# A diffusion trunk on one core: the opening stage taken by quarters of the features instead of halves

## The chip, the cores and the metric

One NeuronCore of a Trainium2 chip runs the whole program. The metric is the device time of one execution in microseconds. TensorE (PE, with its weight loads as PEld), VectorE (DVE), ScalarE (ACT), GpSimd (POOL) and SyncE (SP, which issues the transfers here) each run their own list of instructions in the order in which the kernel writes them.

## The reference

Two layers run over 256 latent and 256 context tokens of 1024 features. Each sub-layer normalises its input, multiplies by a gain that depends on the condition, and adds a shift that depends on it. The first sub-layer is a gated feed-forward block. What the change touches, cut to its core:

```
lat = x + pos_embed ; cx = ctx
mod = silu(cond) @ w_ada[l] + b_ada[l]            # 9 vectors of 1024; 0 is a shift, 1 a scale
h   = rmsnorm(x, g) * (1 + mod[1]) + mod[0]        # for latents (c) and for context (c_ctx)
y   = (silu(h @ w1) * (h @ w3)) @ w2               # w1, w3: 1024 x 2816
x   = x + 0.5 * mod[2] * y
```

## The kernel before

Activations lie features by tokens: eight feature tiles of 128 partitions, 512 tokens wide (latents, then context). Products are made at nearly full float32 accuracy from three passes: `h` and each weight are split into a rounded part (`hi`, by ACT, line 210 for weights) and the rest (`lo`, by DVE, line 214), and `mm3` runs hi*hi (line 309), hi*lo (line 310) and lo*hi (line 311). One pass is one matmul of a 128x128 block on 512 tokens.

A weight item is a block of 512 rows (four feature tiles) by 256 columns. A plan lists all items in order; the function `pump` moves three counters along that list. An item is loaded when one of 3 raw buffers (`wraw`) is free, that is when the item three places before it has been split; it is split when one of 4 pairs `whi`, `wlo` is free, that is when TensorE has finished the item four places before it. Two caps, `cap_load` and `cap_split`, hold the counters back during the opening. Item 0 and item 1 are the first 512 rows of the first column blocks of w1 and w3 (the plan swaps two entries for this), items 2 and 3 the last 512 rows of the same blocks, items 4 and 5 the next column block of w1, items 6 and 7 that of w3. SP issues all transfers one after the other, and each waits for the one eight places before it on SP's list, so at most eight are under way. From a point set by `paces` on, columns of `w_ada` for later sub-layers come along with the weight items and are summed on DVE.

The first shift and scale cannot come that way, since everything waits for them. The function `start` loads their columns itself, in tiles named `a`: eight transfers of 1 MB, four for features 0 to 511 (two for the shift, `j` = 0, two for the scale, `j` = 1) and four for features 512 to 1023. `first_ada` sums one half of one vector on TensorE (line 281, into `ada_ps`), ACT copies the sum (`ada_sb`, line 284), TensorE turns it by a transpose (`ada_t`, line 290), and DVE adds the bias (line 294) and, for the scale, applies the norm's gain (line 299). The reciprocal norm of each token is spread over a diagonal (`tmp`, line 379) and broadcast to all partitions by a matmul with ones (line 386); line 985 copies it to `bcs`. `modulated(half)` then makes `h` for four feature tiles: for each tile, latents then context, DVE multiplies (line 405), ACT adds the shift and rounds (`h_hi`, line 406), DVE takes the rest (`h_lo`, line 395).

The rest of `start`, and the head of `ffn`, hold the first column block of w1 and w3: 32 groups of three passes. They come as w1 with the first half of the features (8 groups), the sums of the second half's scale, w3 with the first half (inside which the sums of the second half's shift and the making of its `h` are called as a task in the background, `second_half`), then, in `ffn`, w1 and w3 with the second half. The four PSUM buffers of the pool `mm` hold the four results (two column tiles of w1, two of w3). When a result of w1 is complete, ACT takes its silu (line 447), which frees the buffer; DVE multiplies with w3's (line 449). `turn` transposes rows of biases and gains into columns; `turn(0)` is needed for the first shift, `turn(1)` not before the second layer.

Of the kernel before, what the change touches and what calls it, by code (L numbers as in the profile page):

```python
# [74 lines left out]
class Trunk:  # L75
# [28 lines left out]
    def plan(self):  # L104
# [32 lines left out]
        paces = {(0, 1): (2, (2, 2, 2, 2, 0)), (0, 2): (4, (2, 1, 2, 1, 2, 0)), (1, 1): (4, (2, 1, 2, 1, 2, 0)),  # L137
                 (1, 2): (4, (1, 0))}
        r = []
        seen = {}  # L140
# [284 lines left out]
    def ffn(self, l, n, both):  # L425
# [6 lines left out]
        with tc.tile_pool(name=f"g{l}{n}", bufs=1) as gp:  # L432
# [31 lines left out]
            if self.begun:  # L464
                hs = self.begun
                self.begun = None
                for part, w in ((1, w1), (3, w3)):
                    it = self.take(w, l, 4, 0)
                    self.fm(it, hs[part], self.h_hi, self.h_lo, BOTH, KT)
                    self.done(it)  # L470
                    gate(hs[part], 0, whole, part)
            elif both:
                its = {0: None}
                up(0, LAT, its, keep=True)
                self.drain()
                up(0, CTXC, its)
            else:
                self.drain()
                up(0, LAT, None)
# [388 lines left out]
    def start(self):  # L868
# [23 lines left out]
        with self.tc.tile_pool(name="start", bufs=1) as st:  # L892
# [33 lines left out]
            def load_ada(half, j):  # L926
                for k in (0, 4):
                    raw = raws[half, j, k] = st.tile([P, 4, 512], F32, tag=f"a{half}{j}{k}", name="a0")
                    c0 = j * D + 512 * half
                    src = io["w_ada"][0, k * P:(k + 4) * P, c0:c0 + 512]  # L930
# [12 lines left out]
            while small:  # L943
                nc.sync.dma_start(*small.pop(0))
            self.cap_load = len(self.ws)
# [1 line left out]

            cond = st.tile([P, KT, 32], F32, tag="cond", name="cond0")
            nc.vector.memset(cond, 0.0)
            bcs = self.wp.tile([P, 2, 512], F32, tag="acc", name="bcs")  # L950
            ss = self.sp.tile([P, 16], F32, tag="ss", name="ss", bufs=3)[:, :2]

            def enter(s, k2):
                a, b = (LAT, CTXC)[s]
                w = SEQ // GRID_W
                ps = (self.aux, self.bank)[s]()
                for k in (k2, k2 + 1):
                    for t in range(2):
                        o = SEQ * (k - k2) + t * P
                        nc.tensor.transpose(ps[:, o:o + P], xs[("x", "ctx")[s]][:, t, k * P:(k + 1) * P], self.ident)  # L960
                if s == 1:
                    nc.scalar.activation(self.x[:, k2:k2 + 2, a:b], ps.rearrange("p (k t) -> p k t", k=2), AF.Copy)
# [10 lines left out]
                for k in (k2, k2 + 1):  # L973
                    self.add_square(k, (a, b))

            def first_ada(half, j):
                self.ada_rows(0, j, half, [(cond[:, k], raws[half, j, 4 * (k // 4)][:, k % 4]) for k in range(KT)])

            def finish_ada():
                later, self.later = self.later, []  # L980
                for f in later:
                    f()

            def row(s, dg):
                nc.vector.tensor_copy(bcs[:, s, :SEQ], self.broadcast(dg))

            def modulated(half):
                for _ in self.modulate(0, 0, [bcs[:, s, :SEQ] for s in range(2)],
                                       [[(s, k) for k in range(4 * half, 4 * half + 4) for s in range(2)]]):
                    pass  # L990

            for k2 in range(0, KT, 2):
                enter(0, k2)
                if k2 == 2:
                    ps = self.bank()
                    nc.tensor.transpose(ps[:, :16], cc, self.ident[:16, :16])
                    nc.scalar.activation(cond[:, :, 0:2], ps[:, :16].rearrange("p (s k) -> p k s", s=2), AF.Silu)
            for k2 in range(0, KT, 2):
                enter(1, k2)
            r = self.token_rstd(LAT)  # L1000
            for t in range(2):
                nc.scalar.activation(bcs.rearrange("p s n -> p (s n)"), xs["ctx"][:, t], AF.Square,
                                     accum_out=ss[:, t:t + 1])
            first_ada(0, 0)
            dg = [self.spread(r), self.spread(self.rstd(ss, 2, D))]
            nc.vector.tensor_copy(self.cond, cond[:, :, 0:2])

            def turn(l):
                vr, n = rows[l]
                ps = self.aux()  # L1010
                nc.tensor.transpose(ps[:, :n], vr[:n, :], self.ident[:n, :n])
                nc.vector.tensor_copy(self.vec[l][:, :n], ps[:, :n])

            turn(0)
            row(0, dg[0])
            row(1, dg[1])
            finish_ada()
            self.cap_split = 1
            self.pump()
            first_ada(0, 1)  # L1020
            finish_ada()
            modulated(0)
            self.cap_split = 2

            def second_half():
                first_ada(1, 1)
                finish_ada()
                self.cap_split = 3
                self.pump()
                modulated(1)  # L1030
                self.cap_split = len(self.ws)
                self.pump()
                yield 2
                turn(1)

            hs = {}
            for part in (1, 3):
                if part == 3:
                    first_ada(1, 0)
                    finish_ada()  # L1040
                    self.behind(second_half())
                hs[part] = [self.bank(), self.bank()]
                it = self.take(f"ffn1_w{part}", 0, 0, 0)
                self.fm(it, hs[part], self.h_hi, self.h_lo, BOTH, KT)
                self.done(it)
            self.begun = hs

    def final(self):
        nc = self.nc
# [56 lines left out]
```

## Time and profile before

| what | value |
|---|---|
| three runs | 1787.40, 1790.61, 1796.05 us, median 1790.61 |
| the profiled execution's own time | 1787.99 us |
| its span in the trace | 1786.2 us, so 1.8 us lie around it |
| TensorE busy | 1753.0 us, 98% |
| DVE, ACT busy | 63%, 38% |

Busy TensorE is close to the whole span, so what another engine saves is worth nothing unless TensorE waits for it. The three runs lie 8.7 us apart, 0.5% of the time.

### The profile page before, as it was taken

What the parts mean: (1) busy time and instruction counts of PE and PEld (TensorE: products, weight loads), DVE (VectorE), ACT (ScalarE), POOL (GpSimd) and SP (SyncE); (2) the same over time, 40 slices, a digit from 0 to 9 for tenths busy, and PEclk for the clock granted to TensorE, in tenths of its full rate; (3) what the DMA queues carried; (4) which work ended last, traced back from release to release, by engine and by line L of the source; (5) the groups of instructions that cost most, each with busy time, mean ns of one, the idle gap of its engine ahead of it and who ended that gap; (6) DMA issues with size and microseconds to landing.
All of it is one profiled execution on the core that took longest, in us unless ns stands there. A gap on an engine that the chain in (4) does not pass through costs nothing. (4 is left out here: it accounts for less than half of the span.)

```text
span 1786.2 us, 27050 instructions
## 1 busy us (share of the span) xinstructions
PE 1753.0 (98%) x10853; PEld 1534.5 (86%) x10853; DVE 1129.6 (63%) x1746; ACT 670.5 (38%) x1087; POOL 19.6 (1%) x26
## 2 busy tenths in 40 slices
PE   6999999999999999999999999999999999989998
PEld 5788888899899898888888898888888999979998
DVE  4876676775737667666666676555545668665554
ACT  3422222236545344222222252223222565545543
POOL 0000000000000000000000000000000000000000
PEclk9999999999999999999999999999999999989999
DMA  8565655664212114555555545555454532446663
GB/s 315 166 177 162 178 160 165 180 188 139 71 60 83 60 60 144 151 157 160 151 153 158 178 137 157 161 154 159 156 167 153 160 107 83 130 125 195 194 186 128
DMA packets 230646, 266.65 MB, mean 149 GB/s; under 512 B 10369, under 2 KB 192377, under 8 KB 230521
## 3 DMA queue, kind: packets, MB, share of 16 engines
q1 hardware_dynamic: 230520, 264.93, 48.8%
q8 instruction: 85, 1.39, 0.3%
q14 instruction: 41, 0.33, 0.1%
HBM read 263.84 MB, written 1.05 MB: 148 GB/s over the span
## 5 line engine op out<-in xcount | busy, mean ns | idle before, releaser
L309 PE MATMUL mm<-h_hi,whi 128*128 128x512 f32 (+1 forms) x2016 | 704.2, 349 | 4.7 <-ACT h_hi L406 3.0
L310 PE MATMUL mm<-h_lo,whi 128*128 128x512 f32 (+1 forms) x2016 | 696.8, 346 | 1.7 <-DVE h_lo L395 1.4
L311 PE MATMUL mm<-h_hi,wlo 128*128 128x512 f32 (+1 forms) x2016 | 694.1, 344 | 0.0
L214 DVE TENSOR_TENSOR wlo<-wraw,whi 128x1024 fp32r<-128x1024 f32 x362 | 430.8, 1196 | 320.0 <-ACT whi L210 318.9
L210 ACT ACTIVATE whi<-wraw 128x1024 fp32r<-128x1024 f32 x362 | 370.9, 1032 | 393.3 <-PE mm L310 271.5
L309 PEld LDWEIGHTS mm<-h_hi,whi 128*128 128x128 f32 x2016 | 380.5, 189 | 56.3 <-ACT h_hi L406 4.0
L310 PEld LDWEIGHTS mm<-h_lo,whi 128*128 128x128 f32 x2016 | 380.8, 189 | 50.7 <-DVE h_lo L395 6.0
L311 PEld LDWEIGHTS mm<-h_hi,wlo 128*128 128x128 f32 x2016 | 380.7, 189 | 47.2
L272 DVE SCALAR_TENSOR_TENSOR acc<-wada,cond,acc 128x512 f32<-128x512 f32 x392 | 275.7, 748 | 35.5 <-DMA wada<-in_w_ada_dram 33.9
L309 PE MATMUL mm<-g_hi,whi 128*128 128x256 f32 (+1 forms) x836 | 279.9, 335 | 0.0
L311 PE MATMUL mm<-g_hi,wlo 128*128 128x256 f32 (+1 forms) x836 | 276.7, 331 | 0.0
L310 PE MATMUL mm<-g_lo,whi 128*128 128x256 f32 (+1 forms) x836 | 276.7, 331 | 0.0
L309 PEld LDWEIGHTS mm<-g_hi,whi 128*128 128x128 f32 x836 | 157.3, 188 | 18.3 <-issue 2.4
L311 PEld LDWEIGHTS mm<-g_hi,wlo 128*128 128x128 f32 x836 | 157.2, 188 | 15.8
L310 PEld LDWEIGHTS mm<-g_lo,whi 128*128 128x128 f32 x836 | 157.1, 188 | 15.2
L210 ACT ACTIVATE g_hi<-silu 128x512 fp32r<-128x512 f32 (+1 forms) x92 | 51.7, 562 | 179.2 <-DVE silu L449 179.2
L447 ACT ACTIVATE silu<-mm 128x512 f32<-128x512 f32 (+1 forms) x92 | 48.2, 527 | 134.3 <-PE mm L311 134.3
L214 DVE TENSOR_TENSOR g_lo<-silu,g_hi 128x512 fp32r<-128x512 f32 (+1 forms) x92 | 55.7, 606 | 57.8 <-ACT g_hi L210 57.8
L449 DVE TENSOR_TENSOR silu<-silu,mm 128x512 f32<-128x512 f32 (+1 forms) x92 | 55.0, 598 | 28.6 <-PE mm L311 28.5
L309 PE MATMUL mm<-whi,h_hi 128*128 128x256 f32 x224 | 64.0, 286 | 0.0
L310 PE MATMUL mm<-wlo,h_hi 128*128 128x256 f32 x224 | 62.3, 278 | 0.0
L311 PE MATMUL mm<-whi,h_lo 128*128 128x256 f32 x224 | 62.2, 278 | 0.0
(128 smaller groups left out, 1055.1 us busy)
## 6 DMA issues: line engine op xcount, KB each, us to landing
wraw<-in_ffn_w_dram SPq DMA_DIRECT2D x271, 512.0 KB, 4.5
wada<-in_w_ada_dram SPq DMA_DIRECT2D x256, 256.0 KB, 3.0
wraw<-in_w_in_dram SPq DMA_DIRECT2D x56, 512.0 KB, 4.0
a<-in_w_ada_dram SPq DMA_DIRECT2D x8, 1024.0 KB, 9.8
wraw<-in_w_out_dram SPq DMA_DIRECT2D x16, 512.0 KB, 4.1
wraw<-in_ffn_w_dram SPq DMA_DIRECT2D x19, 256.0 KB, 2.7
x<-in_x_dram SPq DMA_DIRECT2D x2, 512.0 KB
ctx<-in_ctx_dram SPq DMA_DIRECT2D x2, 512.0 KB, 5.6
```

The costliest lines, as they stand in the source:

```text
L210: self.nc.scalar.activation(hi, src, AF.Copy)
L214: self.nc.vector.tensor_tensor(lo, src, hi.bitcast(F32), op=ALU.subtract)
L272: nc.vector.scalar_tensor_tensor(acc[:, s], raw, c, acc[:, s], op0=ALU.mult, op1=ALU.add)
L309: mm(ps, lhsT=l_hi, rhs=r_hi, start=start, stop=False)
L310: mm(ps, lhsT=l_hi, rhs=r_lo, start=False, stop=False)
L311: mm(ps, lhsT=l_lo, rhs=r_hi, start=False, stop=stop)
L447: nc.scalar.activation(silu[j], ps, AF.Silu)
L449: nc.vector.tensor_tensor(silu[j], silu[j], ps, op=ALU.mult)
```

## The change

The columns of the first shift and scale are loaded, summed and applied for two feature tiles at a time: sixteen transfers of 512 KB in four quarters in place of eight of 1 MB in two halves. One sum of TensorE (`quarter_sums`, line 982) now holds shift and scale of a quarter. The products of the first column block are cut along the features, so that all four results grow together: in each quarter 2 groups for the first column tile of w1, the sums of the next quarter, 2 groups for the second tile, the transpose and the making of the next `h`, then 2 and 2 groups for w3. All 32 groups now stand in `start`; `ffn` goes on with the gate. Squares are taken later and those of the context earlier; the broadcast norm is read from PSUM and not copied; `turn` uses a buffer of the pool `mm`, and `turn(1)` follows the last product. The columns for later sub-layers start two weight items later.

```diff
-        paces = {(0, 1): (2, (2, 2, 2, 2, 0)), ...
+        paces = {(0, 1): (4, (2, 2, 2, 2, 0)), ...
...
                 for part, w in ((1, w1), (3, w3)):
-                    it = self.take(w, l, 4, 0)
-                    self.fm(it, hs[part], self.h_hi, self.h_lo, BOTH, KT)
-                    self.done(it)
                     gate(hs[part], 0, whole, part)
...
-            load_ada(0, 0)
-            self.cap_load = 1
-            self.pump()
-            load_ada(0, 1)
-            self.cap_load = 2
-            self.pump()
-            load_ada(1, 0)
-            load_ada(1, 1)
+            for q in range(4):
+                load_ada(q, 0)
+                self.cap_load = q + 1
+                self.pump()
+                load_ada(q, 4)
...
+            def quarter_sums(q):
+                ps = self.adp.tile([P, 512], F32, tag="ada", name="ada_ps")[:, :P]
+                for k in range(KT):
+                    for c in range(4):
+                        rhs = raws[q, c // 2, 4 * (k // 4)][:, k % 4, P * (c % 2):P * (c % 2) + P]
+                        nc.tensor.matmul(ps[32 * c:32 * c + 32, :], lhsT=cond[:, k], rhs=rhs,
+                                         start=(k == 0), stop=(k == KT - 1))
+                sb = self.sp.tile([P, P], F32, tag="ada", name="ada_sb", bufs=1)
+                nc.scalar.activation(sb, ps, AF.Copy)
+                return sb
...
+            turn(0)
+            sb = quarter_sums(0)
             nc.vector.tensor_copy(self.cond, cond[:, :, 0:2])
...
             self.cap_split = 1
             self.pump()
-            first_ada(0, 1)
-            finish_ada()
+            bank = self.aux().rearrange("p (s t) -> p s t", s=2)
+            bc = {}
+            for s in (1, 0):
+                dg = self.spread(r[1 - s])
+                bc[s] = bank[:, s]
+                nc.tensor.matmul(bc[s], lhsT=self.ones, rhs=dg.rearrange("p n t -> p (n t)"), start=True, stop=True)
+            quarter_mods(0, sb)
             modulated(0)
             self.cap_split = 2
...
+            for q in range(4):
+                if q % 2 == 0:
+                    its = {part: self.take(f"ffn1_w{part}", 0, 2 * q, 0) for part in (1, 3)}
+                products(1, 0, q)
+                if q < 3:
+                    sb = quarter_sums(q + 1)
+                products(1, 1, q)
+                if q < 3:
+                    quarter_mods(q + 1, sb)
+                    modulated(q + 1)
+                    self.cap_split = q + 3 if q < 2 else len(self.ws)
+                products(3, 0, q)
+                products(3, 1, q)
+                if q % 2:
+                    self.done(*its.values())
                 self.pump()
+            turn(1)
```

Three places in the lists of instructions matter for what follows. The first is DVE ahead of the first `h`. Of before, with the two spreads (line 379), the copies of the broadcast and the split of item 0 (`wlo_299`):

```order
L352 TENSOR_SCALAR ms_236<-aux_233 128x2 [waits PE_49]
L379 TENSOR_TENSOR tmp_277<-ident_78,r_238 128x256 [waits Pool_49]
L352 TENSOR_SCALAR ms_279<-ss_155 128x2 [waits Activation_49]
L379 TENSOR_TENSOR tmp_283<-ident_78,r_281 128x256 [waits Pool_49]
L1006 COPY cond_87<-cond0_152 128x16
L1012 COPY vec_98<-aux_286 128x128 [waits PE_49]
L985 COPY bcs_154<-aux_289 128x256 [waits PE_49]
L985 COPY bcs_154<-aux_292 128x256 [waits PE_49]
L294 TENSOR_TENSOR mods_96<-ada_t_295,vec_98 128x2x4 [waits PE_49]
L214 TENSOR_TENSOR wlo_299<-wraw_128,whi_298 128x1024 [waits DMAHW6_49,Activation_49]
L294 TENSOR_TENSOR mods_96<-ada_t_343,vec_98 128x2x4 [waits PE_49]
```

Of the changed kernel, the same stretch, where `wlo_302` is the split of item 0:

```order
L352 TENSOR_SCALAR ms_251<-ss_171 128x2
L352 TENSOR_SCALAR ms_258<-aux_255 128x2 [waits PE_49]
L1008 COPY vec_98<-mm_262 128x128 [waits PE_49]
L1026 COPY cond_87<-cond0_168 128x16
L214 TENSOR_TENSOR wlo_302<-wraw_128,whi_301 128x1024 [waits DMAHW6_49,Activation_49]
L379 TENSOR_TENSOR tmp_312<-ident_78,r_253 128x256 [waits Pool_49]
L379 TENSOR_TENSOR tmp_315<-ident_78,r_260 128x256 [waits Pool_49]
L994 TENSOR_TENSOR mods_96<-ada_t_318,vec_98 128x2x2 [waits DVE_49,PE_49]
L994 TENSOR_TENSOR mods_96<-ada_t_318,vec_98 128x2x2
L997 SCALAR_TENSOR_TENSOR mods_96<-mods_96,vec_98 128x2x2 [waits DVE_49]
```

The split of item 0 has moved from behind the spreads to ahead of them, and on ACT its other part (`whi_301`) stands behind the copy of the first quarter's sum.

The second place is ACT at the end of the first column block. Of before, `mm_375` and `mm_376` are the two results of w1, `whi_565` is the split of item 5:

```order
L210 ACTIVATE whi_523<-wraw_302 128x1024 [waits DMAHW5_49]
L210 ACTIVATE whi_529<-wraw_381 128x1024 [waits DMAHW0_49]
L210 ACTIVATE whi_565<-wraw_493 128x1024 [waits DMAHW1_49,PE_49]
L447 ACTIVATE silu_595<-mm_375 128x512 [waits PE_49]
L447 ACTIVATE silu_597<-mm_376 128x512 [waits PE_49]
```

Of the changed kernel, from the last `h_hi` of the fourth quarter on; `whi_593`, `whi_599`, `whi_629`, `whi_635` are items 4 to 7, `mm_343` and `mm_344` the two results of w1:

```order
L406 ACTIVATE h_hi_93<-tmp_572,mods_96 128x256 [waits DVE_49] x2
L210 ACTIVATE whi_593<-wraw_341 128x1024 [waits DMAHW0_49]
L210 ACTIVATE whi_599<-wraw_429 128x1024 [waits DMAHW1_49]
L210 ACTIVATE whi_629<-wraw_513 128x1024 [waits DMAHW2_49,PE_49]
L210 ACTIVATE whi_635<-wraw_597 128x1024 [waits DMAHW3_49,PE_49,Activation_49]
L447 ACTIVATE silu_650<-mm_343 128x512
L447 ACTIVATE silu_652<-mm_344 128x512
```

The silus now stand behind the split of item 7, which waits for its load and for TensorE's last read of item 3.

The third place is TensorE at the same point. Of the changed kernel, `mm_346` is the second result of w3, `whi_593` is item 4, with which the second column block begins:

```order
L310 MATMUL mm_346<-h_lo_94,whi_509 128x512
L311 MATMUL mm_346<-h_hi_93,wlo_510 128x512
L1007 MATMUL mm_641<-ident_78,vr_109 128x104 [waits DMAHW6_49,Activation_49]
L309 MATMUL mm_660<-h_hi_93,whi_593 128x512 [waits Activation_49]
L310 MATMUL mm_660<-h_lo_94,whi_593 128x512
```

Of before, the transpose of `turn(1)` stood in the middle of the products and took a buffer of another pool:

```order
L309 MATMUL mm_445<-h_hi_93,whi_377 128x512
L310 MATMUL mm_445<-h_lo_94,whi_377 128x512
L311 MATMUL mm_445<-h_hi_93,wlo_378 128x512
L1011 MATMUL aux_544<-ident_78,vr_109 128x104 [waits DMAHW7_49,DMAHW5_49,DMAHW1_49]
L309 MATMUL mm_446<-h_hi_93,whi_377 128x512
```

The transpose now takes the `mm` buffer that the first silu frees, and the next block's first product the one that the second silu frees, so both wait for ACT.

## Rows read from the trace of the kernel before

**Rows 1.** Three stages: busy us (count) by engine, clock, DMA share, GB/s

```profile
0.00:27.50 27.50, 14.90 (x172) 11.82 (x173) 11.57 (x37) 11.26 (x25) 2.11 (x8) 0.95 0.95 336
27.50:58.95 31.45, 29.66 (x227) 21.90 (x228) 21.84 (x44) 14.45 (x25) 0.00 (x0) 0.93 0.69 232
58.95:1786.20 1727.25, 1708.46 (x10455) 1500.78 (x10453) 1096.18 (x1666) 644.77 (x1039) 17.53 (x18) 1.00 0.48 145
```

**Rows 2.** Timeline of TensorE, first column block: start us, length us, [idle before]

```profile
27.50 0.80 PE L309 MATMUL mm<-h_hi,whi 128*128 128x512 f32 x1 [1.92 <-ACT h_hi L406]
...
35.90 1.95 PE L281 MATMUL ada_ps<-a,cond 128*32 128x128 f32 x64
...
38.31 0.33 PE L290 MATMUL ada_t<-ident,ada_sb 128*128 128x128 f32 x1 [0.46 <-ACT ada_sb L284]
...
49.43 0.50 PE L310 MATMUL mm<-h_lo,whi 128*128 128x512 f32 x1 [0.63 <-DVE h_lo L395]
...
52.15 0.39 PE L309 MATMUL mm<-h_hi,whi 128*128 128x512 f32 x1
...
58.95 0.39 PE L309 MATMUL mm<-h_hi,whi 128*128 128x512 f32 x1
```

**Rows 3.** Timeline, from the scale's last columns to the first product

```profile
23.57 1.08 PE L281 MATMUL ada_ps<-a,cond 128*32 128x128 f32 x32 [1.73 <-DMA a<-in_w_ada_dram]
24.78 0.28 ACT L284 ACTIVATE ada_sb<-ada_ps 128x128 f32<-128x128 f32 x1 [5.89 <-PE ada_ps L281]
...
25.62 0.17 DVE L294 TENSOR_TENSOR mods<-ada_t,vec 128x8 f32<-128x8 f32 x1 [4.24 <-PE ada_t L290]
...
26.02 1.28 DVE L405 SCALAR_TENSOR_TENSOR tmp<-x,mods,bcs 128x256 f32<-128x256 f32 x3
...
28.01 0.48 DVE L395 SCALAR_TENSOR_TENSOR h_lo<-tmp,mods,h_hi 128x256 fp32r<-128x256 f32 x1
```

**Rows 4.** Timeline, the shift's first half and the broadcast norm

```profile
16.35 1.08 PE L281 MATMUL ada_ps<-a,cond 128*32 128x128 f32 x32 [0.40 <-DMA a<-in_w_ada_dram]
...
17.83 1.06 ACT L210 ACTIVATE whi<-wraw 128x1024 fp32r<-128x1024 f32 x1
18.47 0.43 DVE L379 TENSOR_TENSOR tmp<-ident,r 128x256 f32<-128x256 f32 x1 [0.81 <-POOL r L354]
...
19.04 0.67 PE L386 MATMUL aux<-tmp,ones 128*128 128x256 f32 x2 [0.91 <-DVE cond L1006]
...
19.55 0.27 PE L290 MATMUL ada_t<-ident,ada_sb 128*128 128x128 f32 x1
...
20.09 0.16 DVE L294 TENSOR_TENSOR mods<-ada_t,vec 128x8 f32<-128x8 f32 x1
20.16 1.22 DVE L214 TENSOR_TENSOR wlo<-wraw,whi 128x1024 fp32r<-128x1024 f32 x1
```

**Rows 5.** Stages of 1 us where the clock changes; columns as in Rows 1

```profile
24.00:25.00 1.00, 0.65 (x24) 0.38 (x16) 0.00 (x0) 0.22 (x1) 0.00 (x0) 0.99 1.04 381
25.00:26.00 1.00, 0.48 (x1) 0.18 (x1) 0.33 (x2) 0.05 (x1) 0.00 (x0) 0.50 1.05 389
...
31.00:32.00 1.00, 1.00 (x3) 0.34 (x3) 1.00 (x4) 0.72 (x3) 0.00 (x0) 0.60 1.05 385
```

**Rows 6.** A stage with transfers of 1 MB, and one where smaller ones follow

```profile
27.00:32.00 5.00, 4.25 (x8) 2.24 (x9) 5.00 (x14) 3.59 (x9) 0.00 (x0) 0.52 1.05 385
35.00:38.00 3.00, 2.86 (x69) 2.16 (x67) 0.00 (x0) 0.02 (x1) 0.00 (x0) 1.00 1.09 353
```

**Rows 7.** DMA issues of the page: KB each, median us from issue to landing

```profile
wraw<-in_ffn_w_dram SPq DMA_DIRECT2D x271, 512.0 KB, 4.5
```

**Rows 8.** Groups by line and shape: busy us, mean ns of one

```profile
L447 ACT ACTIVATE silu<-mm 128x512 f32<-128x512 f32 x62 | 37.1, 598 | 119.0 <-PE mm L311 119.0
L405 DVE SCALAR_TENSOR_TENSOR tmp<-x,mods,aux 128x256 f32<-128x256 f32 x72 | 32.8, 476 | 6.7 <-PE aux L386 6.7
...
L405 DVE SCALAR_TENSOR_TENSOR tmp<-x,mods,bcs 128x256 f32<-128x256 f32 x16 | 7.3, 479 | 0.0
```

More of the change, by code (lines that the diff above doesn't have):

```diff
@@ L136, in plan @@
                 for half in range(2) for k in range(KT)]
-        paces = {(0, 1): (2, (2, 2, 2, 2, 0)), (0, 2): (4, (2, 1, 2, 1, 2, 0)), (1, 1): (4, (2, 1, 2, 1, 2, 0)),
+        paces = {(0, 1): (4, (2, 2, 2, 2, 0)), (0, 2): (4, (2, 1, 2, 1, 2, 0)), (1, 1): (4, (2, 1, 2, 1, 2, 0)),
                  (1, 2): (4, (1, 0))}
@@ L924, in load_x, with load_ada @@
                     load(xs[nm][:, t], io[nm][0, t * P:(t + 1) * P, :], after[t])
[L926 to L930, printed above, removed]
+            def load_ada(q, k):
+                for j in range(2):
+                    raw = raws[q, j, k] = st.tile([P, 4, 256], F32, tag=f"a{q}{j}{k}", name="a0")
+                    c0 = j * D + 256 * q
+                    src = io["w_ada"][0, k * P:(k + 4) * P, c0:c0 + 256]
                     load(raw, src.rearrange("(k p) c -> p k c", p=P))
@@ L949, in start @@
             nc.vector.memset(cond, 0.0)
-            bcs = self.wp.tile([P, 2, 512], F32, tag="acc", name="bcs")
+            junk = self.wp.tile([P, 2, 512], F32, tag="acc", name="junk")
             ss = self.sp.tile([P, 16], F32, tag="ss", name="ss", bufs=3)[:, :2]
@@ L972, in enter @@
                                             ps[:, o:o + SEQ].rearrange("p (r c) -> p r c", c=GRID_W), pe, op=ALU.add)
[L973 to L989, printed above, removed]
-                    pass
+                lagged.append(lambda: [self.add_square(k, (a, b)) for k in (k2, k2 + 1)])
+            lagged = []
+            def ctx_square(t):
+                nc.scalar.activation(junk.rearrange("p s n -> p (s n)"), xs["ctx"][:, t], AF.Square,
+                                     accum_out=ss[:, t:t + 1])
@@ new lines, in quarter_mods @@
+            def quarter_mods(q, sb):
+                ps = self.axp.tile([P, 4, 32], F32, tag="x", name="ada_t")
+                nc.tensor.transpose(ps.rearrange("p c b -> p (c b)"), sb, self.ident)
+                for j in range(2):
+                    m = self.mod(0, j)[:, :, 2 * q:2 * q + 2]
+                    bias = self.vec[0][:, 8 * j + 2 * q:8 * j + 2 * q + 2]
+                    nc.vector.tensor_tensor(m, ps[:, 2 * j:2 * j + 2, 0:2].rearrange("p c s -> p s c"),
+                                            bias[:, None, :].to_broadcast([P, 2, 2]), op=ALU.add)
+                g = self.vec[0][:, None, 72 + 2 * q:74 + 2 * q].to_broadcast([P, 2, 2])
+                nc.vector.scalar_tensor_tensor(m, m, 1.0, g, op0=ALU.add, op1=ALU.mult)
@@ L992, in start, with modulated, turn @@
+            def modulated(q):
+                for _ in self.modulate(0, 0, bc,
+                                       [[(s, k) for k in (2 * q, 2 * q + 1) for s in range(2)]]):
+                    pass
+            def turn(l):
+                vr, n = rows[l]
+                ps = self.bank()
+                nc.tensor.transpose(ps[:, :n], vr[:n, :], self.ident[:n, :n])
+                nc.vector.tensor_copy(self.vec[l][:, :n], ps[:, :n])
             for k2 in range(0, KT, 2):
@@ L997, in start @@
                     nc.scalar.activation(cond[:, :, 0:2], ps[:, :16].rearrange("p (s k) -> p k s", s=2), AF.Silu)
+                if k2 >= 4:
+                    ctx_square(k2 // 2 - 2)
+                if k2:
+                    lagged.pop(0)()
+            lagged.pop(0)()
             for k2 in range(0, KT, 2):
                 enter(1, k2)
[L1000 to L1003, printed above, removed]
@@ L1004, in start @@
-            first_ada(0, 0)
-            dg = [self.spread(r), self.spread(self.rstd(ss, 2, D))]
-            nc.vector.tensor_copy(self.cond, cond[:, :, 0:2])
[L1008 to L1016, printed above, removed]
-            finish_ada()
+            r = [self.rstd(ss, 2, D), self.token_rstd(LAT)]
@@ L1018, in start @@
+            turn(0)
+            sb = quarter_sums(0)
+            nc.vector.tensor_copy(self.cond, cond[:, :, 0:2])
             self.cap_split = 1
             self.pump()
-            first_ada(0, 1)
-            finish_ada()
+            bank = self.aux().rearrange("p (s t) -> p s t", s=2)
[4 more added lines that the diff above has]
+                nc.tensor.matmul(bc[s], lhsT=self.ones, rhs=dg.rearrange("p n t -> p (n t)"), start=True, stop=True)
@@ L1022, in start @@
+            quarter_mods(0, sb)
             modulated(0)
             self.cap_split = 2
[L1025 to L1028, printed above, removed]
-                self.pump()
[L1030 to L1045, printed above, removed]
@@ L1046, in start, with products @@
-            self.begun = hs
+            self.pump()
+            self.begun = hs = {part: [self.bank(), self.bank()] for part in (1, 3)}
+            def products(part, j, q):
+                it = its[part]
+                w = slice(P * j, P * j + P)
+                for k in (2 * q, 2 * q + 1):
+                    self.mm3(hs[part][j], it.hi[:, k % 4, w], it.lo[:, k % 4, w], self.h_hi[:, k], self.h_lo[:, k],
+                             k == 0, k == KT - 1)
+            its = {}
+            for q in range(4):
[13 more added lines that the diff above has]
+                    self.done(*its.values())
+                self.pump()
```

## The prediction

> **What bounds the kernel now.** I read three stages of the span first: the time up to the first product, the first column block of 32 groups, and the rest [rows 1]. In the rest TensorE is busy 1708.5 of 1727.3 us, so nothing there can be won by this change, which alters that part only in that the later columns come two weight items later. A microsecond by which the second column block begins sooner or later is a microsecond of the whole. So the only number that counts is the time at which it begins: 58.95 us, the last row of [rows 2]. The reader should see two parts ahead of it: 27.50 us in which no product runs, and 31.45 us in which 32 groups run.
>
> The timeline of TensorE gives the price of the groups. The tenth-last group and the first of the second block start at 52.15 and 58.95 us, ten groups apart [rows 2]: 0.68 us a group, 21.8 us for 32. The block takes 31.45, so 9.65 us are lost in it. The first eight groups take 8.4 us (27.50 to 35.90) in place of 5.4: 3.0 lost, since the clock stood at half (0.50, back at full inside the row that shows 0.60) [rows 5] and `h_lo` was still being made. Two sums with the wait for ACT's copy cost 2.4 each up to the transpose (35.90 to 38.31) [rows 2], 4.8 in all. The other 1.85 are the transposes and waits for `h_lo` of the second half, of which 0.63 at 49.43 is one [rows 2].
>
> What starts the block is a chain: the last columns of the first half's scale land at 23.57, where TensorE had waited 1.73 us for them; ACT copies the sum at 24.78, DVE has the bias at 25.62, the first multiplication at 26.02, the first product at 27.50 [rows 3].
>
> **The change, part one: the first product.** In the kernel before, the first 2.1 MB of columns are the shift's first half, and TensorE stopped waiting for them at 16.35 [rows 4]. Now the first 2.1 MB are a whole quarter, shift and scale, with item 0 (0.52 MB) ahead of the last piece. At 385 GB/s [rows 6] that adds 1.4: the quarter is there at 17.7, 5.9 us sooner than the 23.57 of before. But the chain behind it is longer. From landing to ACT's copy 1.2 as before (23.57 to 24.78) [rows 3], so 18.9; the copy 0.3, then the split of item 0 on ACT, 1.06 [rows 4], to 20.3; its other part on DVE, 1.22 [rows 4], to 21.5; and behind it in DVE's list the two spreads, 0.43 each [rows 4], to 22.4. In the kernel before both the spreads and this split were done while the scale's columns were on their way, so they cost nothing; that cover is gone. Then the matmul with ones 0.14 later and the transpose 0.51 behind its start (19.04 to 19.55) [rows 4], 23.05; the bias 0.54 later (19.55 to 20.09) [rows 4], 23.6; one more small DVE operation, 0.1; then 0.40 to the multiplication and 1.48 to the first product (25.62, 26.02, 27.50) [rows 2, 3]. That makes **25.6 us, 1.9 sooner**. That the multiplication reads PSUM is free: 476 ns against 479 [rows 8]. Bounds: 24.2 if item 0 delays the quarter's last piece by nothing, 26.5 if the half-sized transfers run at 353 GB/s [rows 6] and the matmuls of the chain at half clock.
>
> **Part two: the 32 groups.** 21.8 us of groups stay. Sums: three stand between products now, not two, but the second tile's groups cover ACT's copy, so each costs 1.95 [rows 2] and 0.1 to start: 6.15. Three transposes of 0.3 [rows 2]: 0.9. The start at half clock: I take 2.5, near the 3.0 of before (the 3.0 held eight groups, here only the first two and the sum fall into it). Waits for `h_lo`: the second `h_lo` of a quarter is done 2.5 us behind the first multiplication (26.02 to 28.49) [rows 3] and that 0.75 behind the transpose, 3.2 in all; four groups of w3 and a pass fill 2.95 of it, so TensorE waits 0.3 in each of three quarters, 1.05 with the next tile's. Sum: 21.8 + 6.15 + 0.9 + 2.5 + 1.05 = 32.4. The 32 groups end at **58.0**, where in the kernel before they end at 58.95. Bounds 31.3 (no loss to the clock beyond 1.4) to 33.5. The columns of the later quarters are no limit: 7.45 MB follow the first quarter; at 353 GB/s [rows 6] they are there at 38.8 us, and TensorE asks for the last at 25.6 + 12.2 (18 groups) + 4.1 (two sums) + 2.5 + 1.3 = 45.7.
>
> **Part three: the step to the second block.** This is new. The transpose of `turn(1)` takes the buffer of w1's first result, and the second block's first product that of w1's second result; both are freed by silus, and on ACT the silus stand behind the split of item 7. In the kernel before the silus of w1 came eight groups sooner and TensorE never waited. Item 7's raw buffer comes free when item 4 is split, and `cap_split` lets item 4 be split only behind the making of the last quarter's `h`. That making starts 7.8 us before the last group ends (12 groups of 0.68 and 0.35 of waits less the 0.75 above). Its last `h_hi` is done 2.6 later, item 4's split takes 1.06 on ACT and 1.22 on DVE [rows 4]: the buffer is free 2.9 us before the last group ends. A load takes 4.5 us from issue to landing [rows 7], so item 7 lands 1.6 us behind the last group. Then its split, 1.06 [rows 4], and two silus of 0.6 [rows 8]: TensorE starts again **3.9 us** after its last group. Bounds: 2.3 if the load is there in time (split and silus alone, since the split also waits for TensorE's last read of item 3), 4.8 if a load takes a microsecond more. Behind the silus nothing more is late: the other two `mm` buffers are wanted 2.7 us into the block.
>
> **The sum.** The second block begins at 25.6 + 32.4 + 3.9 = 61.9, 2.95 us later than 58.95. The rest is as before: as many sums and weight items, and DVE with 0.64 of that stage busy [rows 1] has room for columns that come two items later. On the profiled execution, 1787.99 us, that is 1790.9. That execution is 2.6 below the median of the three runs; over all four times the median is 1789.3, and I forecast **1792.2**. What a measurement of this kernel can tell from no change is about 0.5%, 9 us; the runs shown alone lie 8.7 apart.
>
> **Rivals.**
> *No wait at the second block.* If item 7 is there early and ACT reaches the silus as w1's results are complete, part three falls away: 58.0, 0.95 sooner than before, and 2 us more if the clock is still at full speed at the first product. That is 1786.4 to 1788.4. Against it speaks ACT's list, in which the split that waits for TensorE's last read of item 3 stands ahead of the silus. I give 0.13.
> *The clock falls in the gap.* The first gap that the trace shows, 1.73 us up to 23.57 [rows 3], left the clock at 0.99 in the next microsecond, and it fell to 0.50 at 25 us after a stretch of short matmuls and waits [rows 5]. A gap of 3.9 us behind busy work is not in the trace. If the clock falls, about 4 us pass at half speed as from 27.50 on [rows 2, 5], 2.1 us more: the second block in effect 5 us late, 1794.3. I give 0.10. The Trainium skill, "TensorE: Matmul & The Clock Gate", section "HAM oscillation — how this bites in real kernels", says that waits between bursts make the engine start each burst throttled; by that rule this rival holds, and no stretch of this trace shows a gap of that length.
> *Slower by over 0.5%: the smaller transfers starve the sums.* Eight transfers under way are now half as many bytes. The last quarter would have to land 6.1 us later than 45.7, at 51.8, for the time to grow by 9 us: 218 GB/s in place of 353. If the transfers went one at a time, 0.52 MB in 4.5 us [rows 7] is 117 GB/s: the quarter lands at 81, and the time is 1787.99 + 38, some 1827. For it speaks the fall from 385 to 353 where smaller transfers follow [rows 6]; against it that even eight, some of them tiny, hold over 2 MB, which 385 GB/s takes 5 us to move, longer than one landing. I give 0.05. The Trainium skill, "DMA: Bandwidth & Descriptors", section "Measured (HBM→SBUF, 128 partitions, SWDGE, issued from GpSimd)", sets 1 MiB as the size from which a transfer has three quarters of the peak; as an estimate, three quarters of 385 would be 289 GB/s and the last quarter there at 43.5, still in time. The trace's 353 with half-sized ones among them is better than the rule.
> *Faster by over 0.5%* would need the second block at 50 us. With 25.6 and 28.9 us of groups, sums and transposes, and no wait at all, it is 54.5; I give this 0.02.
>
> **How the numbers follow.** My forecast, a second block 0 to 4 us late, has 0.70. The range holds the first rival's 1786.4 and the second's 1794.3, and 4 us for the scatter of a median at its upper side: 1786.5 to 1798. All cases but the third rival and the last lie within 0.5%: faster 0.02, same 0.93, slower 0.05.
>
> **What would show it.** In the trace after: the first product near 25.6, with the spreads behind the split of item 0; TensorE's waits for columns small from the second quarter on; three sums of 2 us between products; the last group near 58.0; a gap of 2 to 5 us before the second block, ended by ACT's silu, with ACT idle ahead of it for a load of `wraw`. I am wrong if the second block begins before 57 or after 67 us, or if TensorE's idle time behind it grows.

## The result and the profile after

The changed kernel takes 1802.25 us (median of 7 runs, 1799.27 to 1806.76) where the kernel before takes 1790.37 (7 runs beside them, 1787.4 to 1796.07). The ratio is 1.0061, with a 95% interval from 1.0041 to 1.0082: slower by 11.9 us, above the forecast of 1792.2 and above its range. The profiled run took 1803.8 us with a span of 1802.0, against 1787.99 and 1786.2. Runs of one kernel here lie in two clusters some 7 us apart, the kernel before too (24 of 31 runs at 1787.6 to 1790.4, seven at 1796.0 to 1797.7), so a median can lie a few us from a single profile.

TensorE's timeline of the changed kernel at the opening and at the second column block; columns: start, duration, engine, line, operation, tiles and shapes, count, and in brackets the wait and what ended it:

```profile
16.01 2.35 PE L982 MATMUL ada_ps<-a,cond 128*32 128x128 f32 x36
18.75 1.92 PE L982 MATMUL ada_ps<-a,cond 128*32 128x128 f32 x28 [0.39 <-DMA a<-in_w_ada_dram]
23.59 2.08 PE L1034 MATMUL aux<-tmp,ones 128*128 128x256 f32 x4 [2.92 <-DVE tmp L379]
25.46 0.42 PE L990 MATMUL ada_t<-ident,ada_sb 128*128 128x128 f32 x1
27.86 0.79 PE L309 MATMUL mm<-h_hi,whi 128*128 128x512 f32 x1 [1.98 <-ACT h_hi L406]
...
59.79 0.39 PE L311 MATMUL mm<-h_hi,wlo 128*128 128x512 f32 x1
62.34 0.31 PE L1007 MATMUL mm<-ident,vr 104*128 104x104 f32 x1 [2.16 <-ACT silu L447]
62.83 0.79 PE L309 MATMUL mm<-h_hi,whi 128*128 128x512 f32 x1 [0.18 <-ACT silu L447]
```

The first product stands at 27.86 (before 27.50), the 32 groups end at 60.0, and the second block begins at 62.83, 3.9 later than the 58.95 of before [rows 2]. ACT at the same place shows what the gap waits for: the split of item 7 waits 2.41 us for its load, and the two silus stand behind it.

```profile
60.75 1.06 ACT L210 ACTIVATE whi<-wraw 128x1024 fp32r<-128x1024 f32 x1 [2.41 <-DMA wraw<-in_ffn_w_dram]
61.71 1.07 ACT L447 ACTIVATE silu<-mm 128x512 f32<-128x512 f32 x2
```

Windows of the same execution (stretch, length, busy us of PE, PEld, DVE, ACT, POOL with counts, granted clock, DMA share, GB/s). TensorE was nearly idle from 14 to 15 and its clock fell behind that, ten microseconds sooner than before [rows 5]; behind the gap at the second block it fell again:

```profile
14.00:15.00 1.00, 0.11 (x1) 0.11 (x1) 0.81 (x3) 1.00 (x3) 0.00 (x0) 1.00 0.97 338
15.00:16.00 1.00, 1.00 (x5) 0.79 (x5) 0.16 (x1) 0.65 (x2) 0.71 (x1) 0.54 1.08 365
62.00:63.00 1.00, 0.48 (x2) 0.31 (x3) 1.00 (x2) 0.78 (x2) 0.00 (x0) 0.93 0.99 342
63.00:64.00 1.00, 1.00 (x3) 0.82 (x4) 0.83 (x3) 0.09 (x1) 0.00 (x0) 0.50 0.23 80
65.00:66.00 1.00, 1.00 (x4) 0.72 (x4) 0.86 (x2) 0.10 (x1) 0.00 (x0) 0.50 1.05 373
```

Both traces hold 3076 groups of three passes, and I compared the start of the n-th group in the two; a group is called late by the difference. The changed kernel's are 4.6 to 5.6 us late from the 40th group to 386 us (5.4 in most of that stretch), about 11.3 from 398 us on, 14.5 in most of the stretch from 1044 to 1375 us and 16.1 at the end. So two thirds of the loss lie far behind the stage that the change was written for. In the view of TensorE's waits (engine, line, what it waited for: us in all, times, longest) one row has grown; first the kernel before, then the changed one:

```profile
PE ada_ps L281 <- DVE acc L272: 0.7, 2, 0.4
```

```profile
PE ada_ps L281 <- DVE acc L272: 6.6, 3, 3.6
```

The row is that of the sums of the later columns. The longest wait comes at the 12th of these sums, which did not wait in the kernel before:

```profile
377.40 0.64 PE L281 MATMUL ada_ps<-acc,sel 128*32 128x128 f32 x16
```

The same sum in the changed kernel, with the product ahead of it and the clock behind it:

```profile
388.43 0.28 PE L311 MATMUL mm<-g_hi,wlo 128*128 128x256 f32 x1
392.32 1.00 PE L281 MATMUL ada_ps<-acc,sel 128*32 128x128 f32 x16 [3.60 <-DVE acc L272]
```

```profile
394.00:398.00 4.00, 4.00 (x23) 4.00 (x23) 0.69 (x1) 0.34 (x2) 0.00 (x0) 0.58 0.86 261
```

The sum stands in TensorE's list between products, so every product behind it is late by the wait. DVE just ahead of it:

```profile
384.33 1.49 DVE L347 TENSOR_TENSOR ssq<-ssq,tmp 128x512 f32<-128x512 f32 x2
385.74 2.73 DVE L272 SCALAR_TENSOR_TENSOR acc<-wada,cond,acc 128x512 f32<-128x512 f32 x4
388.39 1.22 DVE L214 TENSOR_TENSOR wlo<-wraw,whi 128x1024 fp32r<-128x1024 f32 x1
390.09 2.74 DVE L272 SCALAR_TENSOR_TENSOR acc<-wada,cond,acc 128x512 f32<-128x512 f32 x4 [0.49 <-DMA wada<-in_w_ada_dram]
```

Two columns cost DVE 2.73 us, and two more can be loaded only when these have left their buffers. In this stretch the items serve 256 tokens (the products are 128x256), so one takes TensorE about 2.8 us where an item of the stretch before takes 5.5: TensorE came to the sum 3.6 us before DVE had the last columns.

### The profile page after: what moved, and what is told of

Same layout as the page of the kernel before. It is cut to its first block, busy times and chain, and to the rows that moved or that the text cites. A ratio compares the mean times of both kernels' runs of the same rounds, so it can differ in the third digit from the quotient of the medians.

```text
span 1802.0 us, 27059 instructions
## 1 busy us (share of the span) xinstructions
PE 1761.6 (98%) x10853; PEld 1541.1 (86%) x10853; DVE 1127.6 (63%) x1750; ACT 669.6 (37%) x1087; POOL 19.7 (1%) x26
## 3 DMA queue, kind: packets, MB, share of 16 engines
HBM read 263.84 MB, written 1.05 MB: 147 GB/s over the span
## 4 chain that ended last, share of the span: by engine, by line
PE 92%; DVE 4%; DMA 2%; ACT 1%; issue 1%; SPq 0%; POOL 0%; ACTq 0%; DVEq 0%; POOLq 0%
PE mm L309 28%; PE mm L310 28%; PE mm L311 28%; PE aux L546 3%; DMA wada<-in_w_ada_dram 1%; PE ada_ps L281 1%; DVE tmp L405 1%; DVE wlo L214 1%; DVE h_lo L395 1%; DVE acc L272 1%; PE o L626 1%; ACT whi L210 0%; PE ada_ps L982 0%; DMA a<-in_w_ada_dram 0%; DVE x L420 0%
## 5 line engine op out<-in xcount | busy, mean ns | idle before, releaser
L294 DVE TENSOR_TENSOR mods<-ada_t,vec 128x8 f32<-128x8 f32 x32 | 5.3, 166 | 93.1 <-PE ada_t L290 93.1
```

## Experiments

Experiments 1, 2, 3 and 5 are compared with 31 runs of the kernel before (median 1789.3 us), the others with 24 further ones (1789.36). Some expectations count the kernels: the second is that of experiment 2, the third that of experiment 3, the fourth that of experiment 5.

**1. The distribution of the later columns alone.** The kernel before, with one number of the change:

```
-        paces = {(0, 1): (2, (2, 2, 2, 2, 0)), ...
+        paces = {(0, 1): (4, (2, 2, 2, 2, 0)), ...
```

> The kernel before with one number changed: the columns for later sub-layers start at weight item 4 in place of 2. Theory P (the start of the columns alone makes TensorE wait later on, because the last columns of a vector now fall among the half-sized items at the end of the first down projection): slower by 8 to 11 us; in the trace the second block still begins near 59 us, and TensorE waits 3 to 4 us for DVE's sums near 385 us and over 1 us near 1020 us, each followed by about 3.4 us at half clock. Theory O (all of the 12 us comes from the opening and what it leaves behind in weights and clock): within 2 us of before and no such wait.

Measured: 1797.9 us (9 runs, 1794.59 to 1805.87) against 1789.3, ratio 1.0040 [1.0020, 1.0061]. The opening is untouched (products 0.1 us off), and the same three waits appear (waits first, then the timeline), the longest at the same sum, in this trace at 387:

```profile
PE ada_ps L281 <- DVE acc L272: 6.7, 3, 3.8
```

```profile
387.04 1.23 PE L281 MATMUL ada_ps<-acc,sel 128*32 128x128 f32 x16 [3.80 <-DVE acc L272]
```

Groups are 5.7 us late behind it and were level ahead of it. That is more than the wait of 3.8, since the clock read 0.67 from 386 to 390 and 0.91 from 390 to 394. By 1550 us they are 7.8 late. From 1600 on they fall back by 6 us more, but there each product takes 281 ns in place of 276, which the later columns cannot explain: the changed kernel hands them out in the same way and has 276 (see the last section). So the trace puts the price of the distribution at some 7.8 us and the medians at 8.6, with an interval of 3.6 to 10.9. One number of the plan, in a line far from the rewritten stage, makes most of the loss.

**2. The quarters with the old distribution.** The changed kernel, in which twelve items in a row (items 4 to 15) now carry two columns each without a pause, so that from item 12 on the columns go with the same items as before:

```
-        paces = {(0, 1): (4, (2, 2, 2, 2, 0)), ...
+        paces = {(0, 1): (4, (2,) * 12 + (0, 2, 2, 2, 2) * 10), ...
```

> The changed kernel with the columns for later sub-layers placed as before from weight item 12 on (twelve items in a row carry two each, then the old pattern of five). Theory P: the waits near 390 and 1028 us go, and what is left is the opening: second block at 62 to 63 us and half clock behind it, 5 to 6 us slower than before, span near 1792. Theory O: still 11 to 15 us slower than before.

Measured: 1792.69 us (12 runs, 1791.59 to 1802.95), ratio 1.0028 [1.0012, 1.0043]: 3.4 above the kernel before. The waits for `acc` are back at 0.7 and the second block begins at 62.88, as theory P has it. The loss is smaller than the 5 to 6 us expected: groups are 5.5 to 5.7 late in most of the stretch up to 1430 us and 4.0 behind 1580. Loss 1 (8.6) and loss 2 (3.4) add up to 12.0, and the whole change costs 11.9; so close a fit is partly luck, since the intervals are 3.6 to 10.9 and 2.1 to 7.7 us.

**3. The later sums one weight item later.** In `ada_sum` of the changed kernel:

```
-            self.later.append(lambda: self.ada_rows(l, j, half, ...))
+            rows = lambda: self.ada_rows(l, j, half, ...)
+            self.later.append(lambda: self.later.append(rows))
```

> The changed kernel, its pace kept, with TensorE's sum of the columns (line 281) called one weight item later. Theory P, with the cause being that TensorE reaches this sum before DVE has the last columns: the waits near 390 and 1028 us vanish or fall under 0.5 us, the time is 5 to 7 us over before. If the cause were another (the transfers themselves late for the weights), the waits move to another line and the time stays 12 us over before.

Measured: 1796.66 us (9 runs, 1795.4 to 1803.47), ratio 1.0039 [1.0021, 1.0057]. Only partly as expected: the waits near 1028 and 1402 are gone, but at 394 one of 2.54 is left, the clock behind it reads 0.57 from 394 to 398, and groups are still 5.5 us later behind it than ahead of it (10.1 and 4.6). One item later shortened the longest wait by 1.1 us and no more.

**4. Two items later.** The same edit with one more `later` around it:

> The changed kernel with the sums of later columns by TensorE two weight items later (the third kernel had them one later, and one wait of 2.5 us near 392 us was left). Theory that all that is lost behind the opening is TensorE ahead of VectorE's columns in the stretch of half-size items: the wait near 392 goes too, waits of L281 for acc are under 0.5 us in all, nothing falls in the clock there, and products behind 400 us stand 5 to 6 us later than in the kernel before (the opening's share), so total 1793.5 to 1795. Rival, that the distribution of columns costs time in another way (transfers that take bandwidth from weights): waits of L281 go, but the shift still grows to 9 us or more by 400 us.

Measured: 1816.19 us (4 runs), ratio 1.0149 [1.0128, 1.0170]. Neither theory foresaw this. TensorE's waits for `acc` are gone, but others take their place: groups are 3.8 late at 75 us and 29.8 at the end. DVE's waits say why; first that of experiment 3, then of this one:

```profile
DVE acc L270 <- PE ada_ps L282: 89.1, 26, 4.9
```

```profile
DVE acc L270 <- PE ada_ps L282: 218.9, 29, 10.3
```

In the kernel before:

```profile
DVE acc L270 <- PE ada_ps L281: 38.2, 18, 3.2
```

The columns of the next half go into the `acc` that TensorE has not read yet, so DVE stands still up to 10.3 us with everything queued behind that instruction: TensorE now waits 8.6 us for sums of squares (before 5.2), 4.1 for `wlo` and 7.8 for `ada_sb` (before 1.4). The sum can come too soon for DVE's columns, and too late for its next ones.

**5. The silus ahead of the last split.** The kernel of experiment 2, with items 6 and 7 split behind the silus (the added line stands in `ffn` behind the two gates) and the transpose of `turn(1)` in an `aux` buffer:

```
-                    self.cap_split = q + 3 if q < 2 else len(self.ws)
+                    self.cap_split = q + 3 if q < 2 else 6
...
+                self.cap_split = len(self.ws)
...
-                ps = self.bank()
+                ps = (self.bank, self.aux)[l]()
```

> As the run with the old pace, and at the end of the first column block the silus of w1 stand ahead of the splits of items 6 and 7 on ACT, with the last transpose in another PSUM pool. Theory G (ACT's order alone makes the 2.8 us gap ahead of the second block, and the gap alone makes the clock fall behind it): no gap over 0.3 us, no half clock near 63 us, second block at about 60.1 us; 1 us over before, span near 1787.3. If the gap came from the late load of item 7 by itself, it stays.

Measured: 1791.27 us (12 runs, 1786.07 to 1796.85), ratio 1.0003 [0.9986, 1.0021], which that scatter doesn't tell from 1789.3; the profile says more. The gap is gone, products run on, and the clock stays at full:

```profile
58.40 0.39 PE L311 MATMUL mm<-h_hi,wlo 128*128 128x512 f32 x1
58.63 0.25 PE L1008 MATMUL aux<-ident,vr 104*128 104x104 f32 x1
58.66 0.48 PE L309 MATMUL mm<-h_hi,whi 128*128 128x512 f32 x1
```

```profile
63.00:66.00 3.00, 3.00 (x15) 2.50 (x14) 2.74 (x4) 2.33 (x3) 0.00 (x0) 1.00 0.06 11
```

The second block begins at 58.66, 4.2 sooner than in the changed kernel. The gap is 2.8 of that; the other 1.4 come from the opening, whose code the edit doesn't touch (the first product stands at 26.10 here and at 27.86 there). Groups stay within 1.2 us of the kernel before up to 1590 us, and the 6.1 by which they are late at the end are the slower products of the last section again. The edit mends ACT's order and the transpose's buffer together; what each would do alone is not shown.

**6. Products in the gap.** The kernel of experiment 2, with ten unused products of 512 columns ahead of `turn(1)`:

```
+            fill = self.aux()
+            for n in range(10):
+                nc.tensor.matmul(fill, lhsT=its[1].hi[:, n % 4, :P], rhs=self.h_hi[:, n % 4], start=True, stop=True)
             turn(1)
```

> The second kernel (quarters, old distribution of later columns), with ten extra matrix products of 512 columns, whose result is not used, put ahead of the second transposition of vectors, where TensorE waited 2.3 us for ScalarE and its clock then read 0.50 for some 3.4 us. They fill 2.3 to 2.5 us. Theory that the fall of the clock is the gap's second cost: the granted clock stays near full from 62 to 67, the second block ends about 1.7 us sooner, and the total is 1 to 2 us under the second kernel's 1792.7. Rival, that the clock falls for another reason: half clock at 63 to 66 as before, total the same or up to 0.5 us more.

The clock of experiment 2 first, then this one's timeline and clock:

```profile
63.00:66.00 3.00, 3.00 (x8) 2.35 (x9) 2.17 (x5) 0.68 (x2) 0.00 (x0) 0.51 0.55 167
```

```profile
58.28 2.43 PE L1068 MATMUL aux<-h_hi,whi 128*128 128x512 f32 x10
62.34 0.31 PE L1007 MATMUL mm<-ident,vr 104*128 104x104 f32 x1 [1.63 <-ACT silu L447]
62.83 0.50 PE L309 MATMUL mm<-h_hi,whi 128*128 128x512 f32 x1 [0.18 <-ACT silu L447]
```

```profile
63.00:66.00 3.00, 3.00 (x14) 2.44 (x15) 2.12 (x5) 0.73 (x2) 0.00 (x0) 1.00 0.77 246
```

The clock holds, 14 products run in the 3 us in place of 8, and the 40th group is 4.0 us late in place of 5.7: the clock's fall costs 1.7. The block still begins at 62.83 though its groups ended at 58.28: ACT and the load of item 7 set that time, as in part three. The total doesn't show the 1.7: 1793.04 us (10 runs), ratio 1.0016 [1.0002, 1.0030], and 1.7 is less than the width of that interval (0.4 to 5.4 us above the kernel before). In the two profiles it is lost near 1575 us. Both kernels wait 1.66 us for ACT there; behind the wait the clock reads 1.00 in experiment 2's profile and 0.83 in this one's (from 1570 to 1580 us; 0.83 in the kernel before too), so experiment 2's lateness falls from 4.9 to 4.0 and this one's rises from 3.5 to 4.1. Why the clock falls in one and not in the other is open.

**7. Spreads and first split ahead of the sums.** Experiment 5's kernel, with one more reordering:

```
+            dg = [self.spread(r[1]), self.spread(r[0])]
+            self.cap_split = 1
+            self.pump()
             sb = quarter_sums(0)
-            self.cap_split = 1
-            self.pump()
```

> The fourth kernel with one more reordering in the opening: the first weight item's split and both spread operations stand ahead of the first quarter's sums instead of behind them. In the trace after, the split (1.05 us) and the lower part (1.23) and the spreads (0.75) ran from 20.9 to 23.9 one behind the other, since ScalarE held them behind the copy of the sums, and TensorE waited 2.92 us for the spreads. Theory that part one was lost on this chain: the first product comes about 2.5 us sooner than in the fourth kernel, with the landing of the first quarter at 18.75 unchanged, and the second block at 56.5 to 57.5; total some 2 us under the fourth kernel and 2 to 4 us under the kernel before. Rival, that later columns hold the quarters behind it: the first product comes sooner, the second block doesn't move, total as in the fourth kernel.

```profile
18.15 1.07 PE L983 MATMUL ada_ps<-a,cond 128*32 128x128 f32 x28 [1.18 <-DMA a<-in_w_ada_dram]
19.15 1.13 PE L1035 MATMUL aux<-tmp,ones 128*128 128x256 f32 x4
20.11 0.27 PE L991 MATMUL ada_t<-ident,ada_sb 128*128 128x128 f32 x1
22.36 0.51 PE L309 MATMUL mm<-h_hi,whi 128*128 128x512 f32 x1 [1.98 <-ACT h_hi L406]
```

Measured: 1783.14 us (12 runs, 1781.62 to 1789.79) against 1789.36, ratio 0.9965 [0.9954, 0.9976]: the fastest of the study, with the next: 6.2 below the kernel before, where the changed one is 11.9 above it. The first product comes at 22.36, 3.7 sooner than in experiment 5 (26.10), more than the 2.5 expected, since the wait of 2.92 for the spreads is gone and the clock was still at full, so that the broadcast took 1.13 in place of 2.08. The quarter landed at 18.15 here and at 17.86 there. The second block begins at 54.62, 4.3 sooner than in the kernel before and sooner than the 56.5 to 57.5 expected. The two profiles, 1784.98 and 1787.99 us, differ by 3.0, half of what the medians do.

**8. Products that hold the clock.** The last kernel with unused products of 128 columns, seven ahead of the sums of squares' broadcast and eight behind the first transpose:

```
+            fill(7)
             r = [self.rstd(ss, 2, D), self.token_rstd(LAT)]
...
             quarter_mods(0, sb)
+            fill(8)
             modulated(0)
```

> The kernel with early spreads plus unused products that keep TensorE at work in its two waits of the opening: seven of 128 columns ahead of the sums of squares' broadcast (where it idled 1.83 us at 13.1 to 14.9 and the clock read 0.50 from 15 on), eight behind the first quarter's transposition. Theory that the half clock is a term of part one: the clock reads 1.00 at 15 to 20, the first product comes 1.0 to 2 us sooner than with early spreads alone, the first block's first groups run at full clock (some 1.5 us more), and the second block begins 2 to 3.5 us sooner. Rival, that the columns' landing sets the pace of every quarter: clock up, but quarter two's sums then wait for their columns, and the second block moves by under 1 us.

```profile
22.33 0.49 PE L309 MATMUL mm<-h_hi,whi 128*128 128x512 f32 x1 [0.19 <-ACT h_hi L406]
24.81 1.29 PE L983 MATMUL ada_ps<-a,cond 128*32 128x128 f32 x36
27.12 1.07 PE L983 MATMUL ada_ps<-a,cond 128*32 128x128 f32 x28 [1.02 <-DMA a<-in_w_ada_dram]
29.61 0.27 PE L991 MATMUL ada_t<-ident,ada_sb 128*128 128x128 f32 x1
```

Measured: 1783.82 us (7 runs, 1782.18 to 1785.08), ratio 0.9964 [0.9950, 0.9978], no different from 1783.14. The rival was right: the clock read 1.00 throughout, the second quarter's sums began 1.0 sooner, waited 1.02 for their columns, and the second transpose stands at 29.61 where it stood at 29.62. The seven products had nothing to mend in this comparison: in experiment 7's trace the clock read 1.00 from 15 to 23 us without them, and the first product stands at 22.33 for 22.36. So what the half clock ahead of the first product costs is not tested here; the traces put it at 0.1 to 0.9 us (part one below).

## Why the prediction was wrong, point by point

**The step that failed** is the one priced at nothing: "The rest is as before: as many sums and weight items, and DVE with 0.64 of that stage busy [rows 1] has room for columns that come two items later." Alone it costs 8.6 us of the 11.9 by the medians and 7.8 by the trace (experiment 1), and without it 3.4 are left (experiment 2). The mean load of DVE says nothing of it: what counts is the one stretch in which items are half as long, and where in it a half of columns ends. The count of columns by item is the same work at another place; TensorE waits for the sum in its own order, and the clock behind the wait adds to it (groups 5.4 us late ahead of the stretch and 11.2 behind it, 5.8 in all for the 3.60). The prediction's own last sentence named this as a way to be wrong, idle time behind the second block, but no rival had a price for it. "Slower by over 0.5%" had 0.05, for transfers that starve the sums; the measured 0.6% came another way.

That experiment 2's 3.4 lie near the 2.95 forecast for the opening is partly luck. In the changed kernel's trace the terms missed by +2.26 (part one), -0.2 (part two), -1.1 (part three) and +1.7 (the clock), which with the 2.95 makes 5.6 in effect; in experiment 2's trace 1.7 of its 5.7 are gained back between 1430 and 1580 us.

**Part one** was mis-sized: 27.86 for 25.6, outside its bound of 26.5. The quarter was there at 18.75 for 17.7 (+1.05). The rest of the sums took 1.97 to the copy for 1.2 (+0.77) and broadcast and transpose 1.59 for 0.65 (+0.94), both at half clock; split and spreads 3.15 for 3.5 (-0.35), the last steps 2.40 for 2.55 (-0.15). Sum +2.26. That the spreads lost their cover behind the split was right, and experiment 7 won it back. The half clock at the sums stood in the bound alone; no term said what keeps TensorE busy ahead of them.

Most of this miss belongs to this execution. Six traces have the same code ahead of the first product (the changed kernel and experiments 2 to 6). In them the quarter lands at 17.86 to 18.75 and the first product stands at 26.10 to 27.86, so 0.5 of the 2.26 is common to all; they share the broadcast at half clock (2.08). In the three late ones (26.88, 27.54 and 27.86: experiments 3 and 2 and the changed kernel) TensorE had waited 1.66 to 1.83 us for the sums of squares just before 15 us, the clock read 0.54 to 0.70 from 15 to 16, and the first product came 8.4 to 9.1 behind the landing. In the others it had waited 0.61 to 1.03, the clock read 1.00 up to 19, and the first product came 8.2 behind the landing. So the early half clock costs 0.1 to 0.9, and a landing that is later by up to 0.9 makes the rest. The rate of the transfers does not explain the landing: from 16 to 19 us it was 346 to 349 GB/s in the changed kernel and 342 to 347 in experiment 5, whose quarter landed at 17.86.

**Part two** was right: 32.4 forecast, 27.86 to 60.0 is 32.2 (31.9 to 33.0 in the traces of experiments 2 to 8).

Two sums of the prediction are off without effect. The columns behind the first quarter, with three weight items, are 7.86 MB and not 7.45, which at the prediction's rate is there at 40.0 us and not 38.8; and 1787.99 + 38 is 1826, not 1827.

**Part three** was right in its mechanism, and experiments 5 and 6 and the rows of ACT show it: the silus behind item 7's split, ended by that item's load. Its size was 2.8 us for 3.9, since the load landed at 60.75, 0.7 behind the last group, not 1.6.

**The clock rival** held (I gave it 0.10): half clock from 63 to 66, forecast 2.1, measured 1.7 (experiment 6). The Trainium skill's page "TensorE: Matmul & The Clock Gate", section "HAM oscillation — how this bites in real kernels", says that waits for transfers between bursts make each burst start throttled. This case's trace agrees in part: 0.50 behind a wait of 2.16 and one of 0.18 us, but 1.00 behind one of 1.63 and one of 0.18 (experiment 6). In effect the second block was 3.9 + 1.7 = 5.6 late, against 2.95 forecast, or 5.0 with that rival.

**The transfers** starved nothing behind the first quarter: the 512 KB pieces moved at 339 to 349 GB/s from 16 to 33 us, some 0.90 of the 385 of before [rows 6], and in the changed kernel no sum waits for its columns from the second quarter on. The page "DMA: Bandwidth & Descriptors" of the Trainium skill, section "Measured (HBM→SBUF, 128 partitions, SWDGE, issued from GpSimd)", asks for transfers of 1 MiB or more for three quarters of the peak. Here pieces of half that size kept 0.90 of the rate of pieces of 1 MB; the measurement decides.

**Faster by over 0.5%** I gave 0.02, as it needed a second block at 50. With its order mended and the old distribution, the second block begins at 54.62, and the gain is 0.35%. That the prediction's 54.5 for no wait at all lies beside it is chance: it is made of 25.6 and 28.9, where the trace has 22.36 and 32.2.

## What to carry to other kernels

When work of one engine is handed out by a count of another engine's items, translate the count into time at every stretch where the items' length changes, and look there at who needs the result, before a shift by two items is called free. A sum that is read later keeps its buffer longer: see what is written into that buffer next. And when a stage is cut into smaller pieces, what used to hide behind the long wait (here spreads and a split) must be moved ahead of the shorter one, or the chain behind the data gets longer than the wait that was saved.

## What the runs showed of the hardware

The length of a wait alone did not tell whether the clock would fall. In the changed kernel TensorE was busy 0.07 and 0.11 of the microseconds from 13 to 15 us, and the clock read 1.00 there and 0.54 and then 0.50 behind them. At the second block it read 0.50 behind waits of 2.16 and 0.18 us (changed kernel) and 1.00 behind waits of 1.63 and 0.18 us that followed 2.43 us of extra products (experiment 6). And behind the same wait of 1.66 or 1.67 us for ACT near 1570 us it read, from 1570 to 1580 us, 0.83 in the kernel before and in experiment 6 and 1.00 in experiment 2. Holding the clock up was worth 1.7 us at the second block, where TensorE sets the pace, and nothing where the second quarter's columns set it (experiment 8).

In the profiles of experiments 1 and 5 the products of 256 columns behind 1600 us take 281 ns each, at a granted clock of 1.00, where they take 276 in the kernel before: some 6 us over that stretch. The edits are unlikely to be the cause, since the changed kernel has experiment 1's distribution of columns, experiment 2 has experiment 5's, and both show 276 from 1650 on; what is, stays open.
